# Matmuls of an iota tile under the first loads, a norm gain applied where transposes are copied out, and a first weight chunk loaded in halves

## The chip, the cores and the metric

One NeuronCore of a Trainium2 chip runs the kernel. The metric is the device time of one execution in microseconds. Engines: PE is TensorE (matmuls and transposes), DVE is VectorE, ACT is ScalarE, POOL is GpSimd, and SP mainly issues DMAs. PEld is TensorE loading weights, which overlaps its matmuls. Each engine works through its own queue in order; semaphores make one wait for another.

## The reference

One decoder layer on x of 512 x 1024 in float32. Only its first lines bear on this change:

```python
def rms_norm(x, g):
    xf = x.astype(jnp.float32)
    y = xf * lax.rsqrt(jnp.mean(xf * xf, axis=-1, keepdims=True) + EPS)
    return (y * g.astype(jnp.float32)).astype(x.dtype)

xn = rms_norm(x, norm1_g)
proj = xn @ w_in
(q, k_c, v_c, k_s, v_s, k_w, v_w, g_nsa, conv_b, conv_c, conv_x, gate_a, gate_b) = jnp.split(proj, SPLIT_POINTS, axis=-1)
...
x = x + mixed @ w_out
h = rms_norm(x, norm2_g)
return x + jnp.square(jax.nn.relu(h @ w_up)) @ w_down
```

Behind the projection come sparse attention in three branches, a gated short convolution and a feed-forward part; the change does not touch them.

## The kernel before

The 512 rows of x are four chunks of 128 (`xs[0]` to `xs[3]`). A chunk is normed (`norm_chunk`): ACT squares it and sums along the row, DVE and ACT make 1/sqrt of the mean, and DVE multiplies x by that number and by `g1b`, which is `norm1_g` loaded once into every partition. Then `transpose_chunk` turns it on TensorE, 128 x 128 at a time, into two PSUM banks of four tiles each (`ptr`; the pool has two such buffers). Each bank is copied out twice: ACT writes the rounded high part `xh`, DVE the remainder `xl` = value − `xh`.

Weights come in chunks of 128 x 1024 through the class `Weights`: `load_to` issues the DMA on SP's queue, `split_step` makes half a chunk's high part `w_hi` on ACT or its remainder `w_lo` on DVE. A product is three matmuls (`mm3`): high times high, high times low, low times high.

The first product gives q, chunk by chunk of x: for c = 0 to 3, over four weight chunks (kp = 0 to 3) of two k-tiles each, so 24 matmuls of 512 columns into one PSUM tile `acc`. In the middle of chunk c, behind kp = 1, the code puts the transposes of chunk c + 1 and then the norm of chunk c + 2. Nothing reorders this: the order in the code is the order in each engine's queue. Where two engines read the same PSUM bank, the framework that builds the program makes the later instruction wait for the earlier one.

After the four chunks TensorE goes on with the fifth weight chunk (trace name `acc<-xh,w_hi`) and with the rest of the layer. The line numbers of the profile before are those below; L87 and L89 are the weights' split, L201 and L202 the root and reciprocal, L214 the Square, L218 the scaling, L228 the transposes, L230 and L231 the copies, L237 to L239 the three matmuls.

Of the kernel before, what the change touches and what calls it, by code (L numbers as in the profile page):

```python
# [29 lines left out]

C_POSK, C_POSV, C_GQ, C_GK, C_CW = 0, 16, 32, 33, 36
C_QS, C_SL, C_DD, C_DR, C_DC, C_MK, C_ID = 60, 68, 76, 588, 1100, 1228, 1356
C_ALL = 1484


class Weights:
# [21 lines left out]
    def load_to(self, i):  # L58
        while self.nl <= min(i, len(self.plan) - 1):
            e = self.plan[self.nl]  # L60
            n = e.shape[1]
            t = self.raw.tile([P, WMAX], F32, name="w_raw", tag="w_raw")
            self.nc.sync.dma_start(t[:, :n], e)
            self.loaded[self.nl] = t[:, :n]
            self.nl += 1

# [35 lines left out]
        return self.parts[i]  # L102


def layer(tc, flat, sizes, x, cst, wck, wcv, g1, g2, out):
    nc = tc.nc
    top = ExitStack()

    def pool(name, bufs=1, psum=False, side=None, dram=False):
        kw = dict(name=name, bufs=bufs, reuse_waits="tile")  # L110
        if psum:
            kw["space"] = PSUM
        if dram:
# [79 lines left out]
    junk = sp.tile([P, DM], F32, name="junk")  # L193
    st1 = cp.tile([P, NT], F32, name="st1")
    xh = xtp.tile([P, NKO, S], F32R, name="xh")
    xl = xtp.tile([P, NKO, S], F32R, name="xl")

    def rms_scale(dst, ss, n):

        nc.vector.tensor_scalar(dst, ss, 1.0 / n, EPS, op0=ALU.mult, op1=ALU.add)  # L200
        nc.scalar.activation(dst, dst, AF.Sqrt)  # L201
        nc.vector.reciprocal(dst, dst)  # L202

    def norm_chunk(c):
        ss = st1[:, c : c + 1]
        if c == 0:
            nc.scalar.activation(junk[:, :512], xs[c][:, :512], AF.Square, accum_out=ss)
            nc.vector.tensor_tensor_reduce(
                junk[:, 512:], xs[c][:, 512:], xs[c][:, 512:], 1.0, 0.0,
                op0=ALU.mult, op1=ALU.add, accum_out=warm,  # L210
            )
            nc.vector.tensor_tensor(ss, ss, warm, ALU.add)
        else:
            nc.scalar.activation(junk, xs[c], AF.Square, accum_out=ss)  # L214
        rms_scale(ss, ss, DM)
        for b in range(2):
            v = slice(b * 512, b * 512 + 512)
            nc.vector.scalar_tensor_tensor(  # L218
                xs[c][:, v], xs[c][:, v], ss, g1b[:, v], op0=ALU.mult, op1=ALU.mult
            )  # L220

    def transpose_chunk(psp, src, hi, lo, c):

        for kk in range(2):
            pt = psp.tile([P, 4, P], F32, name="ptr", tag="tr")
            for k in range(4):
                ko = 4 * kk + k
                nc.tensor.transpose(pt[:, k, :], src[:, ko * P : (ko + 1) * P], ident)  # L228
            h = hi[:, 4 * kk : 4 * kk + 4, c * P : (c + 1) * P]
            nc.scalar.activation(h, pt, AF.Copy)  # L230
            nc.vector.tensor_tensor(  # L231
                lo[:, 4 * kk : 4 * kk + 4, c * P : (c + 1) * P], pt, h.bitcast(F32), ALU.subtract
            )

    def mm3(ps, a, b, start, stop, **kw):

        nc.tensor.matmul(ps, a[0], b[0], start=start, stop=False, **kw)  # L237
        nc.tensor.matmul(ps, a[0], b[1], start=False, stop=False, **kw)  # L238
        nc.tensor.matmul(ps, a[1], b[0], start=False, stop=stop, **kw)  # L239
# [106 lines left out]
    pos = [0]  # L346
# [175 lines left out]
    acc = kv_gemm(ci)  # L522
# [24 lines left out]
    acc = kv_gemm(ci)  # L547
# [308 lines left out]
    ps_acc, close_ps_acc = pool("ps_acc3", 4, psum=True, side="left")  # L856
# [456 lines left out]
```

## Time and profile before

| what | value |
|---|---|
| median of 3 runs | 793.21 us (793.15 to 794.42) |
| profiled execution, whole | 794.31 us |
| its span | 792.5 us |
| TensorE busy | 777.7 us, 98% of the span |
| ACT busy, DVE busy, POOL busy | 394.0, 575.4, 88.2 us |

A row of the trace in order of time gives start, duration, engine, line, operation, what is written and read, the shape and how many; the bracket behind it is the idle time of the engine before it and what ended that. A row of a group gives total busy time and the mean of one in ns. Idle time of an engine that nothing waits for costs nothing.

### The profile page before, as it was taken

To read this page: it belongs to the slowest core of one execution; us is meant where nothing else is said; L and a number is where in the kernel's file an instruction comes from. 1 tells how busy PE (TensorE), PEld (TensorE's weight loads), DVE (VectorE), ACT (ScalarE), POOL (GpSimd) and SP (SyncE) were. 2 spreads that over 40 slices of the span, in tenths; PEclk is the share of its full clock that TensorE was granted. 3 is DMA by queue.
4 is the path that set the end of the run, shared out by engine and by line. 5 is a ranking of instruction groups with operands and counts; after the bars stand their busy time and mean duration, and the time that the engine had idled before them with its cause. 6 is when DMAs were issued, how large, how long until landed. Compare 5 with 4: busy or idle time off the path is not lost.

```text
span 792.5 us, 11860 instructions
## 1 busy us (share of the span) xinstructions
PE 777.7 (98%) x4413; PEld 675.5 (85%) x4413; DVE 575.4 (73%) x968; ACT 394.0 (50%) x714; POOL 88.2 (11%) x139
## 2 busy tenths in 40 slices
PE   5999999999999999999999999999999999999998
PEld 4899888888888888888888889987998899889987
DVE  6587787766667466666556668997699579967984
ACT  5545645545555453222233366973565356535641
POOL 0011573233324100000000000000000000000000
PEclk9999999999999999999999999999999999999999
DMA  9346687658757849998999923649999985655562
GB/s 343 124 132 207 171 172 172 212 134 179 194 160 148 175 127 328 310 318 319 336 340 332 357 96 109 228 161 278 264 276 249 274 254 183 199 184 191 189 206 80
DMA packets 49307, 172.56 MB, mean 218 GB/s; under 512 B 5473, under 2 KB 5857, under 8 KB 49249
## 3 DMA queue, kind: packets, MB, share of 16 engines
q1 hardware_dynamic: 42624, 148.14, 54.6%
q0 software_dynamic: 4608, 16.78, 13.5%
q10 hardware_dynamic: 2016, 6.88, 2.5%
q8 instruction: 35, 0.57, 0.3%
q14 instruction: 24, 0.19, 0.1%
HBM read 152.90 MB, written 52.43 MB: 259 GB/s over the span
## 4 chain that ended last, share of the span: by engine, by line
PE 88%; ACT 5%; DVE 3%; DMA 2%; issue 2%; SPq 0%; DVEq 0%; ACTq 0%
PE acc L237 16%; PE acc L239 15%; PE acc L238 15%; PE dacc L237 6%; PE dacc L238 6%; PE dacc L239 6%; PE uacc L237 4%; PE uacc L239 4%; PE uacc L238 4%; PE sc L645 2%; PE ptu L693 2%; ACT w_hi L87 2%; PE uz L239 1%; PE uz L238 1%; PE uz L237 1%
## 5 line engine op out<-in xcount | busy, mean ns | idle before, releaser
L89 DVE TENSOR_TENSOR w_lo<-w_raw,w_hi 128x512 fp32r<-128x512 f32 (+3 forms) x268 | 233.2, 885 | 73.7 <-ACT w_hi L87 73.1
L87 ACT ACTIVATE w_hi<-w_raw 128x512 fp32r<-128x512 f32 (+3 forms) x268 | 201.4, 779 | 91.5 <-PE dacc L239 63.5
L237 PE MATMUL acc<-xh,w_hi 128*128 128x512 f32 x336 | 136.5, 406 | 0.0
L239 PE MATMUL acc<-xh,w_lo 128*128 128x512 f32 x336 | 131.5, 391 | 0.0
L238 PE MATMUL acc<-xl,w_hi 128*128 128x512 f32 x336 | 131.3, 391 | 0.0
L237 PE MATMUL dacc<-w_hi,uh 128*128 128x512 f32 (+1 forms) x228 | 88.0, 386 | 1.1 <-DVE x L1141 1.1
L238 PE MATMUL dacc<-w_lo,uh 128*128 128x512 f32 (+1 forms) x228 | 88.0, 386 | 0.0
L239 PE MATMUL dacc<-w_hi,ul 128*128 128x512 f32 (+1 forms) x228 | 87.9, 385 | 0.0
L239 PEld LDWEIGHTS acc<-xh,w_lo 128*128 128x128 f32 x336 | 63.1, 188 | 14.1
L237 PEld LDWEIGHTS acc<-xh,w_hi 128*128 128x128 f32 x336 | 63.2, 188 | 9.1 <-issue 0.3
L238 PEld LDWEIGHTS acc<-xl,w_hi 128*128 128x128 f32 x336 | 63.3, 188 | 8.2
L237 PE MATMUL uacc<-hA,w_hi 128*128 128x256 f32 x192 | 53.7, 280 | 0.4 <-DVE a L1029 0.4
L657 ACT ACTIVATE p<-p,nst 128x512 f32<-128x512 f32 (+2 forms) x48 | 29.5, 615 | 48.9 <-DVE nst L653 48.7
L238 PE MATMUL uacc<-hA,w_hi 128*128 128x256 f32 x192 | 53.5, 279 | 0.0
L239 PE MATMUL uacc<-hA,w_lo 128*128 128x256 f32 x192 | 53.5, 279 | 0.0
L237 PEld LDWEIGHTS dacc<-w_hi,uh 128*128 128x128 f32 x228 | 42.8, 188 | 10.1 <-ACT w_hi L87 1.5
L238 PEld LDWEIGHTS dacc<-w_lo,uh 128*128 128x128 f32 x228 | 42.8, 188 | 8.7 <-DVE w_lo L89 0.2
L239 PEld LDWEIGHTS dacc<-w_hi,ul 128*128 128x128 f32 x228 | 42.8, 188 | 8.5
L699 DVE TENSOR_TENSOR pt<-ptu,pt 128x384 fp32r<-128x384 f32 (+1 forms) x48 | 28.9, 601 | 21.0 <-ACT pt L698 20.7
L1141 DVE TENSOR_TENSOR x<-x,dacc 128x512 f32<-128x512 f32 (+1 forms) x57 | 36.7, 670 | 9.8 <-PE dacc L239 9.8
L674 POOL TENSOR_SCALAR p<-p,nst 128x512 f32<-128x512 f32 (+2 forms) x48 | 31.9, 673 | 79.6 <-DVE nst L672 45.3
L300 POOL DMA_DIRECT2D td<-w_flat x8 | 6.5, 843 | 304.2 <-DMA td<-w_flat 304.2
(227 smaller groups left out, 1665.8 us busy)
## 6 DMA issues: line engine op xcount, KB each, us to landing
w_raw<-w_flat SPq DMA_DIRECT2D x110, 512.0 KB, 4.8
w_raw<-tu SPq DMA_DIRECT2D x32, 512.0 KB, 4.8
w_raw<-td SPq DMA_DIRECT2D x32, 512.0 KB, 4.7
tu<-w_flat SPq DMA_DIRECT2D x16, 512.0 KB, 6.2
z<-w_flat SPq DMA_DIRECT2D x16, 512.0 KB, 7.0
tu<-w_flat POOLq DMA_DIRECT2D x8, 512.0 KB, 7.7
tu<-tu POOLq DMA_DIRECT2D x8, 512.0 KB, 8.4
td<-w_flat SPq DMA_DIRECT2D x8, 512.0 KB, 5.4
```

Source lines behind the costliest of these rows:

```text
L87: nc.scalar.activation(hi[:, v], t[:, v], AF.Copy)
L89: nc.vector.tensor_tensor(lo[:, v], t[:, v], hi[:, v].bitcast(F32), ALU.subtract)
L237: nc.tensor.matmul(ps, a[0], b[0], start=start, stop=False, **kw)
L238: nc.tensor.matmul(ps, a[0], b[1], start=False, stop=False, **kw)
L239: nc.tensor.matmul(ps, a[1], b[0], start=False, stop=stop, **kw)
L300: nc.gpsimd.dma_start(h[k], h[m], accum_op=ALU.add)
L645: nc.tensor.matmul(ps[:, : b - a], QS[h][:, t], ks[h // 4][:, a:b], start=k == 0, stop=k == 1)
L657: later(1, lambda: nc.scalar.activation(p, p, AF.Exp, scale=-1.0, bias=mn, accum_out=sm))
L674: nc.gpsimd.tensor_scalar(p_of(u, k), p_of(u, k), nst[:, u % 4, 1, k : k + 1], 1.0, op0=ALU.mult, op1=ALU.mult,)
L693: nc.tensor.transpose(pt[:, n : n + P], p_of(u, c)[:, k * P : (k + 1) * P], ident)
L699: later(1, lambda: nc.vector.tensor_tensor(ptl[:, at], pt[:, :n], pth[:, at].bitcast(F32), ALU.subtract))
L1141: nc.vector.tensor_tensor(v, v, ps[:, o : o + n], op)
```

## The change

- Six matmuls of a tile `busy`, filled by an iota on POOL, run on TensorE ahead of the first transposes. Their result is not used.
- `g1b` and its load are gone. `norm1_g` comes as eight columns beside the identity matrix (`ident_g1`); ko-th column, one number per partition. Since a transposed tile has the model dimension on the partitions, the gain is now a scalar per partition: `gain` copies each 128 x 128 tile out by itself, ACT with `scale=g`, DVE as v·g − `xh`.
- The scaling by the norm alone stays on DVE for chunk 0 (`norm_first`, with the mean and EPS folded into other instructions) and goes to POOL for chunks 1 to 3.
- The first weight chunk is loaded in two halves, and its split is interleaved with the copies of chunk 0.
- The transposes of chunk 1 stand behind kp = 2 of chunk 0 instead of kp = 1.

```diff
+    busy = sp.tile([P, 256], mybir.dt.int32, name="busy")
+    nc.gpsimd.iota(busy, [[17749, 256]], base=1065353216, channel_multiplier=7001)
+    busy = busy.bitcast(F32)
...
-    nc.sync.dma_start(g1b, g1.partition_broadcast(P))
-    nc.scalar.dma_start(ident, cst[:, C_ID : C_ID + P])
+    nc.scalar.dma_start(ident_g1, cst[:, C_ID:])
...
+    idle = ps_acc.tile([P, 512], F32, name="acc", tag="acc")
+    for _ in range(6):
+        nc.tensor.matmul(idle[:, :256], busy[:, :P], busy, start=True, stop=True)
...
+        nc.scalar.activation(ss, ss, AF.Sqrt, scale=1.0 / DM, bias=warm)
+        nc.vector.reciprocal(ss, ss)
+        for b in range(2):
+            v = xs[0][:, b * 512 : b * 512 + 512]
+            nc.vector.tensor_scalar(v, v, ss, None, op0=ALU.mult)
...
-            nc.vector.scalar_tensor_tensor(
-                xs[c][:, v], xs[c][:, v], ss, g1b[:, v], op0=ALU.mult, op1=ALU.mult
-            )
+            nc.gpsimd.tensor_scalar(v, v, ss, 1.0, op0=ALU.mult, op1=ALU.mult)
...
-            h = hi[:, 4 * kk : 4 * kk + 4, c * P : (c + 1) * P]
-            nc.scalar.activation(h, pt, AF.Copy)
-            nc.vector.tensor_tensor(
-                lo[:, 4 * kk : 4 * kk + 4, c * P : (c + 1) * P], pt, h.bitcast(F32), ALU.subtract
-            )
+    def gain(pt, c, kos):
+        t = slice(c * P, (c + 1) * P)
+        for ko in kos:
+            v, g, h = pt[:, ko % 4, :], g1t[:, ko : ko + 1], xh[:, ko, t]
+            nc.scalar.activation(h, v, AF.Copy, scale=g)
+            nc.vector.scalar_tensor_tensor(
+                xl[:, ko, t], v, g, h.bitcast(F32), op0=ALU.mult, op1=ALU.subtract
+            )
...
+    norm_first()
+    pt = [transposed(xs[0], kk) for kk in range(2)]
+    for b in range(2):
+        W.split_step()
+        W.split_step()
+        gain(pt[0], 0, (2 * b, 2 * b + 1))
...
     W.split_to(1)
+    gain(pt[1], 0, range(4, NKO))
     norm_chunk(1)
     W.split_to(3)
...
-            if kp == 1 and c + 1 < NT:
-                transpose_chunk(ps_tr, xs[c + 1], xh, xl, c + 1)
+            if kp == (1 if c else 2) and c + 1 < NT:
+                transpose_chunk(c + 1)
```

ACT's queue from the first weights to the norm of chunk 2, before (the brackets name the semaphores that a row waits for, x_122 is chunk 1, x_123 chunk 2, st the norm's numbers, junk the Square's output):

```order
L87 ACTIVATE w_hi<-w_raw 128x512 [waits DMAHW4_49]
L87 ACTIVATE w_hi<-w_raw 128x512
L230 ACTIVATE xh<-ptr 128x4x128 [waits PE_49] x2
L87 ACTIVATE w_hi<-w_raw 128x512 [waits DMAHW5_49]
L87 ACTIVATE w_hi<-w_raw 128x512
L214 ACTIVATE junk,st_152<-x_122 128x1024 [waits DMAHW6_49,Activation_49]
L201 ACTIVATE st_152<-st_152 128x1 [waits DVE_49]
L87 ACTIVATE w_hi<-w_raw 128x512 [waits DMAHW7_49]
L87 ACTIVATE w_hi<-w_raw 128x512
L87 ACTIVATE w_hi<-w_raw 128x512 [waits DMAHW0_49]
L87 ACTIVATE w_hi<-w_raw 128x512
L230 ACTIVATE xh<-ptr 128x4x128 [waits PE_49] x2
```

The first part of the same stretch now (L89 is the weights' split, L245 the copy, L227 the Square):

```order
L89 ACTIVATE w_hi<-w_raw 128x512 [waits DMAHW2_49]
L245 ACTIVATE xh<-ptr,ident_g_134 128x128 [waits DMAHW3_49,PE_49]
L245 ACTIVATE xh<-ptr,ident_g_134 128x128 [waits DVE_49]
L89 ACTIVATE w_hi<-w_raw 128x512 [waits DMAHW4_49]
L245 ACTIVATE xh<-ptr,ident_g_134 128x128 [waits DVE_49] x2
L89 ACTIVATE w_hi<-w_raw 128x512 [waits DMAHW5_49]
L89 ACTIVATE w_hi<-w_raw 128x512
L245 ACTIVATE xh<-ptr,ident_g_134 128x128 [waits PE_49]
L245 ACTIVATE xh<-ptr,ident_g_134 128x128 [waits DVE_49] x3
L227 ACTIVATE junk,st_152<-x_122 128x1024 [waits DMAHW6_49]
L204 ACTIVATE st_152<-st_152 128x1 [waits DVE_49]
```

A bank's single copy has become four, and every copy but the first of a bank waits for DVE's part of the tile before; the Square of chunk 1 now stands behind all eight.

TensorE's queue where chunk 1 is transposed, now (L256 to L258 are the three matmuls, L237 the transposes, x_122 chunk 1):

```order
L256 MATMUL acc<-w_hi,xh 128x512 [waits Activation_49]
L257 MATMUL acc<-w_lo,xh 128x512 [waits DVE_49]
L258 MATMUL acc<-w_hi,xl 128x512
L237 MATMUL ptr<-ident_g_134,x_122 128x128 [waits DMAHW6_49,Pool_49]
L237 MATMUL ptr<-ident_g_134,x_122 128x128 x3
L237 MATMUL ptr<-ident_g_134,x_122 128x128 [waits Pool_49]
L237 MATMUL ptr<-ident_g_134,x_122 128x128 x3
L256 MATMUL acc<-w_hi,xh 128x512 [waits Activation_49]
```

And before, at the same transposes:

```order
L239 MATMUL acc<-w_hi,xl 128x512
L228 MATMUL ptr<-ident,x_122 128x128 [waits DMAHW6_49,DVE_49,PE_49]
L228 MATMUL ptr<-ident,x_122 128x128 x3
L228 MATMUL ptr<-ident,x_122 128x128 [waits DVE_49,PE_49]
L228 MATMUL ptr<-ident,x_122 128x128 x3
L237 MATMUL acc<-w_hi,xh 128x512 [waits Activation_49]
```

They now wait for POOL instead of DVE, and six more matmuls stand ahead of them.

More of the change, by code (lines that the diff above doesn't have):

```diff
@@ L32 @@
 C_QS, C_SL, C_DD, C_DR, C_DC, C_MK, C_ID = 60, 68, 76, 588, 1100, 1228, 1356
-C_ALL = 1484
+C_G1 = C_ID + P
+C_ALL = C_G1 + NKO
 class Weights:
@@ L62, in load_to @@
             t = self.raw.tile([P, WMAX], F32, name="w_raw", tag="w_raw")
-            self.nc.sync.dma_start(t[:, :n], e)
+            for v in [slice(0, 512), slice(512, n)] if self.nl == 0 else [slice(0, n)]:
+                self.nc.sync.dma_start(t[:, v], e[:, v])
             self.loaded[self.nl] = t[:, :n]
@@ L102, in get, with layer @@
         return self.parts[i]
-def layer(tc, flat, sizes, x, cst, wck, wcv, g1, g2, out):
+def layer(tc, flat, sizes, x, cst, wck, wcv, g2, out):
     nc = tc.nc
@@ L165, in layer @@
     xs = [sp.tile([P, DM], F32, name=f"x{c}") for c in range(NT)]
-    g1b = sp.tile([P, DM], F32, name="g1b")
+    busy = sp.tile([P, 256], mybir.dt.int32, name="busy")
+    nc.gpsimd.iota(busy, [[17749, 256]], base=1065353216, channel_multiplier=7001)
+    busy = busy.bitcast(F32)
     cs = qkv.tile([P, C_ID], F32, name="cs")
@@ L173, in layer @@
     qkv.tile([P, 56], F32, name="even")
-    ident = cp.tile([P, P], F32, name="ident")
+    ident_g1 = cp.tile([P, P + NKO], F32, name="ident_g1")
+    ident, g1t = ident_g1[:, :P], ident_g1[:, P:]
     warm = cp.tile([P, 1], F32, name="warm")
-    cp.tile([P, 8], F32, name="even")
     nc.vector.memset(warm, 1.0)
@@ L202, in rms_scale, with norm_first @@
         nc.vector.reciprocal(dst, dst)
+    idle = ps_acc.tile([P, 512], F32, name="acc", tag="acc")
+    for _ in range(6):
+        nc.tensor.matmul(idle[:, :256], busy[:, :P], busy, start=True, stop=True)
+    def norm_first():
+        ss = st1[:, 0:1]
+        nc.scalar.activation(junk[:, :512], xs[0][:, :512], AF.Square, accum_out=ss)
+        nc.vector.tensor_tensor_reduce(
+            junk[:, 512:], xs[0][:, 512:], xs[0][:, 512:], 1.0 / DM, EPS,
+            op0=ALU.mult, op1=ALU.add, accum_out=warm,
+        )
[4 more added lines that the diff above has]
+            nc.vector.tensor_scalar(v, v, ss, None, op0=ALU.mult)
@@ L204, in norm_chunk @@
     def norm_chunk(c):
         ss = st1[:, c : c + 1]
[L206 to L210, printed above, removed]
-            )
-            nc.vector.tensor_tensor(ss, ss, warm, ALU.add)
-        else:
-            nc.scalar.activation(junk, xs[c], AF.Square, accum_out=ss)
+        nc.scalar.activation(junk, xs[c], AF.Square, accum_out=ss)
@@ L215, in norm_chunk, with transposed @@
         rms_scale(ss, ss, DM)
         for b in range(2):
-            v = slice(b * 512, b * 512 + 512)
+            v = xs[c][:, b * 512 : b * 512 + 512]
+            nc.gpsimd.tensor_scalar(v, v, ss, 1.0, op0=ALU.mult, op1=ALU.mult)
+    def transposed(src, kk):
+        pt = ps_tr.tile([P, 4, P], F32, name="ptr", tag="tr")
+        for k in range(4):
+            ko = 4 * kk + k
+            nc.tensor.transpose(pt[:, k, :], src[:, ko * P : (ko + 1) * P], ident)
+        return pt
+    def gain(pt, c, kos):
[3 more added lines that the diff above has]
+            nc.scalar.activation(h, v, AF.Copy, scale=g)
@@ L218, in norm_chunk, with transpose_chunk @@
             nc.vector.scalar_tensor_tensor(
-                xs[c][:, v], xs[c][:, v], ss, g1b[:, v], op0=ALU.mult, op1=ALU.mult
+                xl[:, ko, t], v, g, h.bitcast(F32), op0=ALU.mult, op1=ALU.subtract
             )
-    def transpose_chunk(psp, src, hi, lo, c):
+    def transpose_chunk(c):
         for kk in range(2):
[L225 to L228, printed above, removed]
-            h = hi[:, 4 * kk : 4 * kk + 4, c * P : (c + 1) * P]
-            nc.scalar.activation(h, pt, AF.Copy)
-            nc.vector.tensor_tensor(
-                lo[:, 4 * kk : 4 * kk + 4, c * P : (c + 1) * P], pt, h.bitcast(F32), ALU.subtract
-            )
+            gain(transposed(xs[c], kk), c, range(4 * kk, 4 * kk + 4))
@@ L243, in layer @@
     sq = pre.tile([P, 512], F32, name="sq")
-    norm_chunk(0)
-    W.split_to(0)
-    transpose_chunk(ps_tr, xs[0], xh, xl, 0)
+    norm_first()
[4 more added lines that the diff above has]
+        gain(pt[0], 0, (2 * b, 2 * b + 1))
     load_x(2)
@@ L1293 @@
     cst = np.concatenate(
-        [pos(a["cmp_pos_k"][0]), pos(a["cmp_pos_v"][0]), gq, gk, cw, *_constants()], axis=1
+        [pos(a["cmp_pos_k"][0]), pos(a["cmp_pos_v"][0]), gq, gk, cw, *_constants(), a["norm1_g"][0].reshape(NKO, P).T], axis=1
     )
@@ L1302 @@
         "wcv": wc(a["w_cmp_v"][0]),
-        "g1": np.ascontiguousarray(a["norm1_g"][0]),
         "g2": np.ascontiguousarray(a["norm2_g"][0]),
@@ L1309 @@
     with tile.TileContext(nc) as tc:
-        layer(tc, t["w_flat"], sizes, t["x_in"], t["cst"], t["wck"], t["wcv"], t["g1"], t["g2"], out)
+        layer(tc, t["w_flat"], sizes, t["x_in"], t["cst"], t["wck"], t["wcv"], t["g2"], out)
     r = run_bass_kernel_spmd(nc, [arrays], core_ids=[0])
```

## Prediction

> **What bounds the kernel now.** I read the page's busy table first, then the span cut into stretches, then TensorE's waits, then the start in order of time.
>
> ```profile
> PE 777.7 (98%) x4413; PEld 675.5 (85%) x4413; DVE 575.4 (73%) x968; ACT 394.0 (50%) x714; POOL 88.2 (11%) x139
> ...
> 0.00:8.57 8.57, 0.00 (x1) 0.01 (x1) 2.05 (x8) 2.41 (x5) 0.20 (x4) 1.00 0.77 247
> 8.57:18.69 10.12, 9.76 (x40) 7.43 (x41) 9.38 (x17) 8.59 (x17) 0.00 (x0) 1.00 1.02 416
> 18.69:36.83 18.14, 18.14 (x90) 15.17 (x88) 10.84 (x22) 9.41 (x20) 0.00 (x0) 1.00 0.31 115
> 36.83:792.50 755.67, 749.76 (x4286) 652.93 (x4284) 553.11 (x924) 373.59 (x672) 87.97 (x135) 1.00 0.71 217
> ...
> PE ptr L228 <- DVE x L218: 8.6, 1, 8.6
> PE dacc L237 <- DVE x L1141: 1.1, 1, 1.1
> ```
>
> Each stretch gives its length, then busy time of PE, PEld, DVE, ACT and POOL. TensorE is the bound from 18.69 us to the end. It idles 8.57 us before its first transpose; after that the longest single wait is 1.1 us. So the change can win only at the start, at most some 8 us. It can also lose: whatever makes TensorE wait between 18.69 and 36.83 us, where it is 100% busy while ACT and DVE are half idle, is added in full.
>
> The start, in order of time (start, duration, engine, what; in brackets the idle time before):
>
> ```profile
> 5.11 0.69 DVE L208 CUSTOM_DVE_ANT_0 junk<-x 128x512 f32<-128x512 f32 x1 [4.24 <-DMA x<-x_in]
> 5.73 0.08 DVE L208 DVE_READ_ACCUMULATOR2_ANT warm<- 128x1 f32 x1
> 6.30 0.20 ACT L201 ACTIVATE st<-st 128x1 f32<-128x1 f32 x1 [1.65 <-DVE st L200]
> 6.53 0.16 DVE L202 RECIPROCAL st<-st 128x1 f32<-128x1 f32 x1 [0.27 <-ACT st L201]
> 7.76 1.42 DVE L218 SCALAR_TENSOR_TENSOR x<-x,st,g1b 128x512 f32<-128x512 f32 x2 [1.06 <-DMA g1b<-g]
> 8.57 1.97 PE L228 MATMUL ptr<-ident,x 128*128 128x128 f32 x8 [8.57 <-DVE x L218]
> 8.95 1.15 ACT L87 ACTIVATE w_hi<-w_raw 128x512 fp32r<-128x512 f32 x2 [2.45 <-DMA w_raw<-w_flat]
> 9.61 1.29 DVE L89 TENSOR_TENSOR w_lo<-w_raw,w_hi 128x512 fp32r<-128x512 f32 x2 [0.44 <-ACT w_hi L87]
> 12.10 1.05 ACT L214 ACTIVATE junk<-x 128x1024 f32<-128x1024 f32 x1
> ```
>
> DVE waits 1.06 us for g1b, and ACT 2.45 us for the first weights, which come behind g1b on the same queue. The change takes the first wait away and brings the second's end forward.
>
> **The change part by part.** *g1b's load out, weights in halves.* On SP one issue goes and one comes, so the queue is level. Everything behind g1b lands earlier. I give this no term of its own: what uses it is counted below, where ACT and DVE become later than the data.
>
> *The first norm.* The reduction ends at 5.81 us; root 0.20, reciprocal 0.16 and hand-overs of 0.04 give 6.28 us for the first scaling (7.76 before). That scaling is now a tensor_scalar without g; no row has it at 128x512. It lies between 0.21 us (128x96, below) and 0.75 us (L218, half of 1.42 and its overlap); I take 0.5, nearer the wide row. First transposes at 6.8 us instead of 8.57.
>
> *The iota and its six matmuls.* POOL and TensorE are idle there.
>
> ```profile
> L467 POOL MEMSET VC<- 128x256 f32 x1 | 0.3, 306 | 0.0
> L283 POOL TENSOR_TENSOR q_sb<-q_sb,q_ss 128x512 f32<-128x512 f32 x2 | 3.0, 1512 | 39.3 <-DVE q_ss L202 39.3
> 57.87 1.15 PE L472 MATMUL ptr<-wck_t,ka 128*64 128x64 f32 x16
> ```
>
> The iota takes 0.3 to 1.5 us and ends by 2.8 us at the latest. The plain f32 matmuls of L472 stand 0.06 us apart for 64 columns, so 0.24 for 256 columns and 0.5 on a slow clock: six end by 5.8 us, under the cover of the wait for x. They cost nothing unless each takes over 0.65 us; at 0.8 the transposes would be 0.8 us late. What they could buy is the slow start: the eight transposes took 1.97 us at 8.57 and 1.03 us later. I count only part of that, as ACT sets the pace from here.
>
> *The copies out of the transposes* decide the case. Before, a bank (four transposed 128x128 tiles) was copied by one ACT and one DVE instruction of 512 columns. Now each tile has its own ACT instruction (times g, rounded) and DVE instruction (times g, minus the rounded), and by the built order ACT's copy of tile k+1 waits for DVE's of tile k, since both read the same bank. The trace has this pattern already, at L438 and L439:
>
> ```profile
> 44.35 0.68 ACT L438 ACTIVATE QS<-ptr,gq 64x512 fp32r<-64x512 f32 x1 [4.41 <-PE ptr L432]
> 45.84 0.69 ACT L438 ACTIVATE QS<-ptr,gq 64x512 fp32r<-64x512 f32 x1 [0.81 <-DVE QS L439]
> ...
> 45.06 0.74 DVE L439 SCALAR_TENSOR_TENSOR QS<-ptr,gq,QS 64x512 fp32r<-64x512 f32 x1 [0.37 <-ACT QS L438]
> 46.56 0.76 DVE L439 SCALAR_TENSOR_TENSOR QS<-ptr,gq,QS 64x512 fp32r<-64x512 f32 x1 [0.75 <-ACT QS L438]
> ...
> L499 ACT ACTIVATE KC<-ptr,cs 128x64 fp32r<-128x64 f32 x1 | 0.3, 306 | 0.0
> L438 ACT ACTIVATE QS<-ptr,gq 64x512 fp32r<-64x512 f32 x8 | 5.5, 684 | 10.3 <-DVE QS L439 5.4 <-PE ptr L432 4.8
> L500 DVE SCALAR_TENSOR_TENSOR KC<-ptr,cs,KC 128x64 fp32r<-128x64 f32 x1 | 0.3, 274 | 0.0
> L439 DVE SCALAR_TENSOR_TENSOR QS<-ptr,gq,QS 64x512 fp32r<-64x512 f32 x8 | 6.0, 750 | 3.5 <-ACT QS L438 3.4
> ```
>
> They alternate strictly, with hand-overs of 0.03 and 0.04 us. Between 64 and 512 columns ACT goes from 306 to 684 ns, so 0.36 us at 128; DVE from 274 to 750 ns, so 0.34 us. A pair is 0.36 + 0.03 + 0.34 + 0.04 = 0.77 us. The Trainium skill (PSUM — Partial Sum Buffer, "PSUM bank collisions raise a hardware error") says why: two engines, two readers included, must not touch one bank in the same partitions at once, and a scheduler orders them. The rows agree; by this rule the overlap of rival three below is shut out.
>
> *Chunk 0.* ACT's first copy starts at about 7.7 us (0.64 us behind the transposes on a quick clock, 1.1 on the slow one; I take 0.9). ACT then has copy 0, copy 1 (+0.77), a half of w_hi, copy 2 at 9.3; DVE must do that half's w_lo until 10.05 before its part of copy 2, so copy 3 is at 10.43, the next two w_hi end at 11.85, their w_lo (1.29) at 12.6, DVE's part of copy 4 at 12.94, and copies 5, 6, 7 start at 12.98, 13.75, 14.52. The Square of chunk 1, behind them, starts at 14.8 us; before, at 12.10. What is queued behind it is chunk 1's root and then w_hi of the third weights, so TensorE stands:
>
> ```profile
> 14.75 1.33 PE L228 MATMUL ptr<-ident,x 128*128 128x128 f32 x8 [0.18 <-issue]
> ...
> 21.42 1.03 PE L228 MATMUL ptr<-ident,x 128*128 128x128 f32 x8
> 22.05 1.09 ACT L230 ACTIVATE xh<-ptr 128x512 fp32r<-128x512 f32 x2 [1.86 <-PE ptr L228]
> 23.02 1.06 ACT L214 ACTIVATE junk<-x 128x1024 f32<-128x1024 f32 x1
> 24.39 0.20 ACT L201 ACTIVATE st<-st 128x1 f32<-128x1 f32 x1 [0.22 <-DVE st L200]
> 24.83 1.41 DVE L218 SCALAR_TENSOR_TENSOR x<-x,st,g1b 128x512 f32<-128x512 f32 x2
> 27.76 1.03 PE L228 MATMUL ptr<-ident,x 128*128 128x128 f32 x8
> ...
> L674 POOL TENSOR_SCALAR p<-p,nst 128x512 f32<-128x512 f32 x16 | 11.4, 711 | 62.5 <-DVE nst L672 31.3 <-ACT pt L698 12.4 <-ACT w_hi L87 9.6
> L579 DVE TENSOR_SCALAR gates<-gates 128x96 f32<-128x96 f32 x1 | 0.2, 210 | 0.9 <-ACT gates L578 0.9
> ```
>
> The root follows its Square by 1.37 us and ends at 16.4; w_hi is done at 17.0, w_lo at 17.7, and the six matmuls that now stand ahead of chunk 1's transposes (0.23 us each) end at 18.9. POOL's scaling of chunk 1 is ready at 18.1 (14.8 + 1.81 + two of 0.71), so it hides.
>
> *The loop for chunks 2 and 3.* From one set of transposes to the next, TensorE needs 27.76 − 21.42 = 6.34 us. The new chain: transposes to the first copy 0.64; six pair steps 4.62; two steps from an ACT copy to the next ACT instruction without a wait, 0.36 each, 0.72; Square to scaling 1.81; POOL's first half 0.71 (the nearest row) with two hand-overs of 0.05. Sum 8.60 us. Chunk 2's transposes stand in TensorE's queue ahead of half of chunk 1's matmuls, so these wait too. Chunk 2 is transposed at 18.9 + 8.6 = 27.5 and chunk 3 at 36.1 us, against 27.76: 8.3 us late. From there the order is the old one, and the copies of chunk 3 (one per 0.77 us) run ahead of matmuls that start 3.8 us later and use one per 0.69 us. The later stages shift along.
>
> **The sum:** 8.3 us, to 8.4 with a hand-over more. The profiled execution has a span of 792.5 us and 794.31 us in all, 1.1 us over the median of 793.21; against the median the forecast is 801.6 us. Its own range is 800.0 to 803.0 (copy start and POOL 0.6 to 0.8 us either way).
>
> **Rivals.** One: *a smaller loss.* At the 64-column rows the pair is at least 0.306 + 0.274 + 0.07 = 0.65 us. Some 17 pair steps lie on the path (12 in two loops, 5 in chunk 0): 17 × 0.12 = 2.0 less, 799.6 us. If TensorE's 1.1 us wait at L1141 also went, 798.5.
>
> Two: *the clock falls back.* TensorE stands still from about 13.4 to 17.0 us and from 24.3 to 27.5. Cold work costs double in the trace:
>
> ```profile
> 10.63 0.80 PE L237 MATMUL acc<-w_hi,xh 128*128 128x512 f32 x1
> 12.15 0.58 PE L237 MATMUL acc<-w_hi,xh 128*128 128x512 f32 x1
> ```
>
> These two starts, three matmuls apart, lie 1.52 us apart and later 0.69 (some of it a wait). Six matmuls on half the clock add 1.1 us, and four transposes 0.47, in each of two places: 1.1 + 2 × 0.47 = 2.1 us, 803.7 us. The granted clock reads 1.00 in every stretch, so only durations can show it. For it: the gaps are as long as the slow start was (8.57 to 12.2 us). Against it: no row shows a quick TensorE falling back. The Trainium skill (TensorE: Matmul & The Clock Gate, "What's actually happening") has the clock halve after an idle window of about 3.4 us that runs free of the work, and open after one busy window; by that rule a gap of 3.6 us holds a whole window only now and then.
>
> Three: *not slower.* If ACT and DVE worked on one bank side by side, a tile would cost ACT's 0.36 us or less, the loop 0.64 + 8 × 0.36 + 1.81 + 0.81 = 6.1 us, under TensorE's 6.34, and only the start would count. The Square of chunk 1 would start at 7.7 + 8 × 0.36 + 3 × 0.58 (halves of w_hi, L87) = 12.3 us, its transposes 4.1 us behind it as above, at 16.4; level would be 14.75 (where chunk 1 was transposed) + 6 × 0.23 = 16.1. That gives 793.5 us. It decides where a pair costs under (6.34 − 8.60 + 4.62) / 6 = 0.39 us. L438 and L439 speak against it.
>
> **How the numbers follow.** The forecast gets 0.62, the clock 0.17, the smaller loss 0.13, not slower 0.07, anything else 0.01. The range 798.7 to 804.8 takes in rivals one and two with half a microsecond to a microsecond beside them and leaves out rival three. Slower by over 0.2% (1.6 us, about what a measurement here can tell): 0.92; within: 0.05; faster: 0.03, the part of rival three where the start saves more than 1.6 us.
>
> **What would show it.** In the new profile: first transposes near 6.8 us; ACT's copies with "idle <-DVE xl" before them, 0.77 us apart; TensorE waiting for POOL's x twice, about 3 us and 2 us; the first matmul with the fifth weights at about 45 us instead of 36.83; TensorE dense after that. I am wrong if the copies stand 0.4 us apart, if DVE's part is much cheaper than 0.34 us at 128 columns, or if POOL's scaling takes well over 0.71 us.

## The result, and the profile after

| | before | after |
|---|---|---|
| median | 793.18 us (793.11 to 794.42, 4 runs) | 803.91 us (803.53 to 804.14, 4 runs) |
| profiled execution, whole | 794.31 us | 804.14 us |
| its span | 792.5 us | 802.3 us |

After over before is 1.0125, with a 95% interval of 1.011 to 1.014: the change makes the kernel slower, by 9.8 us from profile to profile. The forecast was 801.6, slower, with a range of 798.7 to 804.8.

The busy table of the page:

```profile
PE 788.2 (98%) x4425; PEld 681.3 (85%) x4425; DVE 577.2 (72%) x984; ACT 400.4 (50%) x738; POOL 93.8 (12%) x146
```

TensorE's busy time is up by 10.5 us, though only 12 records are new, with 5.4 us: part of its work must have become slower. The span in stretches says where (length, busy time of PE, PEld, DVE, ACT, POOL, then the granted clock):

```profile
16.75:20.07 3.32, 3.10 (x7) 2.01 (x8) 3.18 (x4) 1.51 (x3) 2.04 (x2) 0.50 1.02 404
20.07:29.00 8.93, 6.80 (x27) 5.48 (x25) 3.06 (x11) 5.04 (x13) 0.74 (x2) 0.81 0.22 74
29.00:37.55 8.55, 8.38 (x32) 6.41 (x32) 3.72 (x12) 5.05 (x13) 1.36 (x3) 0.80 0.01 4
37.55:46.93 9.38, 9.36 (x44) 7.68 (x45) 5.69 (x14) 6.11 (x16) 0.63 (x1) 1.00 0.00 0
46.93:802.30 755.37, 749.81 (x4286) 652.94 (x4284) 554.15 (x926) 373.61 (x672) 88.17 (x135) 1.00 0.72 218
```

The last stretch, from the first matmul with the fifth weights on, has the old length (755.4 against 755.7) and the old busy time of PE: the whole loss lies ahead of 46.93 us, where that matmul stood at 36.83. Two waits of TensorE are new (in all, how many, the longest, in us):

```profile
PE acc L256 <- ACT w_hi L89: 4.2, 3, 3.4
PE ptr L237 <- POOL x L231: 2.3, 2, 2.1
```

The start in order of time, TensorE first:

```profile
1.24 5.41 PE L209 MATMUL acc<-busy 128*128 128x256 f32 x12 [1.24 <-POOL busy L169]
6.50 1.09 PE L237 MATMUL ptr<-ident_g,x 128*128 128x128 f32 x8
16.75 0.80 PE L256 MATMUL acc<-w_hi,xh 128*128 128x512 f32 x1 [3.38 <-ACT w_hi L89]
...
19.21 0.63 PE L257 MATMUL acc<-w_lo,xh 128*128 128x512 f32 x1
19.64 0.63 PE L258 MATMUL acc<-w_hi,xl 128*128 128x512 f32 x1
20.07 1.91 PE L237 MATMUL ptr<-ident_g,x 128*128 128x128 f32 x8
...
29.00 1.33 PE L237 MATMUL ptr<-ident_g,x 128*128 128x128 f32 x8 [2.14 <-POOL x L231]
...
37.55 1.33 PE L237 MATMUL ptr<-ident_g,x 128*128 128x128 f32 x8 [0.15 <-POOL x L231]
46.93 0.39 PE L256 MATMUL acc<-xh,w_hi 128*128 128x512 f32 x1
```

The first transposes are 2 us earlier and quick (1.09 us instead of 1.97). By the third weights all of it is gone: TensorE stands still for 3.38 us, and then works at half pace, matmuls 0.43 us apart instead of 0.23, chunk 1's transposes in 1.91 us. All four runs of the changed kernel read a mean granted clock of 0.991 to 0.993, which fits such a stretch in each of them. ACT and DVE of the same stretch show what it waits for:

```profile
7.25 0.35 ACT L245 ACTIVATE xh<-ptr,ident_g 128x128 fp32r<-128x128 f32 x1
...
14.62 1.05 ACT L227 ACTIVATE junk<-x 128x1024 f32<-128x1024 f32 x1
15.98 0.20 ACT L204 ACTIVATE st<-st 128x1 f32<-128x1 f32 x1 [0.22 <-DVE st L203]
16.09 2.17 ACT L89 ACTIVATE w_hi<-w_raw 128x512 fp32r<-128x512 f32 x4
21.16 0.37 ACT L245 ACTIVATE xh<-ptr,ident_g 128x128 fp32r<-128x128 f32 x1 [2.90 <-PE ptr L237]
21.94 0.37 ACT L245 ACTIVATE xh<-ptr,ident_g 128x128 fp32r<-128x128 f32 x1 [0.42 <-DVE xl L246]
22.73 0.37 ACT L245 ACTIVATE xh<-ptr,ident_g 128x128 fp32r<-128x128 f32 x1 [0.42 <-DVE xl L246]
...
21.56 0.35 DVE L246 SCALAR_TENSOR_TENSOR xl<-ptr,ident_g,xh 128x128 fp32r<-128x128 f32 x1 [1.63 <-ACT xh L245]
22.34 0.35 DVE L246 SCALAR_TENSOR_TENSOR xl<-ptr,ident_g,xh 128x128 fp32r<-128x128 f32 x1 [0.44 <-ACT xh L245]
```

ACT's copies start 0.79 us apart, each idle for 0.42 us on DVE's `xl` and DVE in turn for 0.44 us on `xh`: strict alternation in one bank.

### The profile page after: what moved, and what is told of

It reads as the page before. It is cut to its first block, busy times and chain, and to the rows that moved or that the text cites. A ratio compares the mean times of both kernels' runs of the same rounds, so it can differ in the third digit from the quotient of the medians.

```text
span 802.3 us, 11932 instructions
## 1 busy us (share of the span) xinstructions
PE 788.2 (98%) x4425; PEld 681.3 (85%) x4425; DVE 577.2 (72%) x984; ACT 400.4 (50%) x738; POOL 93.8 (12%) x146
## 4 chain that ended last, share of the span: by engine, by line
PE 86%; ACT 4%; issue 3%; DVE 3%; DMA 2%; POOL 0%; SPq 0%; ACTq 0%; DVEq 0%; POOLq 0%
PE acc L256 15%; PE acc L258 15%; PE acc L257 15%; PE dacc L256 6%; PE dacc L257 6%; PE dacc L258 6%; PE uacc L256 4%; PE uacc L258 4%; PE uacc L257 4%; PE sc L668 2%; PE ptu L716 2%; ACT w_hi L89 1%; PE uz L258 1%; PE uz L256 1%; PE uz L257 1%
## 5 line engine op out<-in xcount | busy, mean ns | idle before, releaser
L89 ACT ACTIVATE w_hi<-w_raw 128x512 fp32r<-128x512 f32 (+3 forms) x268 | 201.2, 779 | 88.5 <-PE dacc L258 62.6
L256 PE MATMUL acc<-xh,w_hi 128*128 128x512 f32 x336 | 136.5, 406 | 0.0
L258 PE MATMUL acc<-xh,w_lo 128*128 128x512 f32 x336 | 131.5, 391 | 0.0
L256 PE MATMUL dacc<-w_hi,uh 128*128 128x512 f32 (+1 forms) x228 | 88.0, 386 | 0.7 <-DVE x L1164 0.7
L258 PE MATMUL dacc<-w_hi,ul 128*128 128x512 f32 (+1 forms) x228 | 87.9, 385 | 0.0
L258 PEld LDWEIGHTS acc<-xh,w_lo 128*128 128x128 f32 x336 | 63.1, 188 | 14.1
L256 PEld LDWEIGHTS acc<-xh,w_hi 128*128 128x128 f32 x336 | 63.2, 188 | 9.2 <-issue 0.3
L256 PE MATMUL uacc<-hA,w_hi 128*128 128x256 f32 x192 | 53.7, 280 | 0.5 <-DVE a L1052 0.5
L258 PE MATMUL uacc<-hA,w_lo 128*128 128x256 f32 x192 | 53.5, 279 | 0.0
L256 PEld LDWEIGHTS dacc<-w_hi,uh 128*128 128x128 f32 x228 | 42.8, 188 | 9.7 <-ACT w_hi L89 1.1
L258 PEld LDWEIGHTS dacc<-w_hi,ul 128*128 128x128 f32 x228 | 42.8, 188 | 8.5
```

What stands on the lines that cost most here:

```text
L89: nc.scalar.activation(hi[:, v], t[:, v], AF.Copy)
```

## The experiments

All are edits of the changed kernel unless said otherwise. This table, put together from the traces, shows the points that the text goes by, in us: first transposes (T0), those of chunks 1 to 3 (T1 to T3), and the first matmul with the fifth weights (W5).

| kernel | T0 | T1 | T2 | T3 | W5 | median | ratio to before, 95% interval |
|---|---|---|---|---|---|---|---|
| before | 8.57 | 14.75 | 21.42 | 27.76 | 36.83 | 793.18 | |
| forecast of after | 6.8 | 18.9 | 27.5 | 36.1 | 45.1 | 801.6 | |
| after | 6.50 | 20.07 | 29.00 | 37.55 | 46.93 | 803.91 | 1.0125, 1.011 to 1.014 |
| wide copies, no gain | 6.69 | 14.34 | 19.31 | 25.66 | 34.72 | 791.87 | 0.9974, 0.9965 to 0.9982 |
| banks in turn | 6.52 | 16.23 | 22.53 | 29.16 | 38.45 | 795.27 | 1.0017, 1.0008 to 1.0026 |
| ACT's four, then DVE's four | 6.74 | 15.72 | 21.04 | 27.66 | 36.72 | 793.54 | 0.9990, 0.9981 to 0.9999 |
| gaps filled, six and three | 6.52 | 18.96 | 27.44 | 36.24 | 45.60 | 802.99 | 1.0113, 1.0097 to 1.0128 |
| gaps filled, seven and seven | 6.77 | 19.14 | 27.63 | 36.16 | 45.50 | 802.97 | 1.0113, 1.0099 to 1.0128 |
| T1 behind kp = 1 | 6.78 | 17.12 | 27.17 | 35.72 | 45.05 | 801.80 | 1.0094, 1.0080 to 1.0108 |
| scaling on DVE | 6.54 | 19.90 | 28.57 | 36.98 | 46.11 | 803.39 | 1.0116, 1.0100 to 1.0131 |
| g's copy by one-row matmuls | 6.95 | 14.81 | 20.10 | 26.45 | 35.51 | 792.21 | 0.9976, 0.9967 to 0.9985 |
| warm-up with one row | 6.82 | 20.44 | 29.37 | 37.91 | 47.26 | 804.23 (one run) | |
| g's copy by full-row matmuls | 8.45 | 15.92 | 21.22 | 27.56 | 36.63 | 794.47 | 1.0002, 0.9994 to 1.0011 |
| g's copy by one-row matmuls, four warm-ups | 8.65 | 16.51 | 21.84 | 28.18 | 37.24 | 793.92 | 0.9994, 0.9984 to 1.0005 |
| the warm-up alone, in the kernel before | 7.80 | 14.00 | 20.67 | 27.01 | 36.08 | 793.28 | 0.9994, 0.9986 to 1.0003 |

The kernel before took 793.88 to 794.25 us (medians) beside these, so ratios compare better than medians. The five points come from one profiled execution of each kernel and can shift between executions by up to three quarters of a microsecond or so: in the last row W5 is 0.75 us earlier than before because `g1b` came in sooner (first scaling at 7.00 instead of 7.76 us), and that edit changes no load.

**Wide copies, no gain.** `gain` becomes one copy a bank and engine.

```diff
-            nc.scalar.activation(h, v, AF.Copy, scale=g)
-            nc.vector.scalar_tensor_tensor(
-                xl[:, ko, t], v, g, h.bitcast(F32), op0=ALU.mult, op1=ALU.subtract
-            )
+        h = xh[:, 4 * kk : 4 * kk + 4, c * P : (c + 1) * P]
+        nc.scalar.activation(h, pt, AF.Copy)
+        nc.vector.tensor_tensor(
+            xl[:, 4 * kk : 4 * kk + 4, c * P : (c + 1) * P], pt, h.bitcast(F32), ALU.subtract
+        )
```

> The changed kernel, but each bank of four transposed tiles is copied by one ACT and one DVE instruction of 512 columns, as before the change; norm1_g is left out, all else stays. Theory A (the alternation tile by tile in one bank is the cost): in the chunk loop the Square follows the transposes by 1.6 us again (21.42 to 23.02 before the change), scaling 1.8 later, POOL's half 0.7, so 4.2 us against TensorE's 6.34, and TensorE sets the pace. Chunk 0: ACT needs about 3.4 us from 7.25 for two copies and four halves of w_hi, Square of chunk 1 near 10.7, chunk 1's transposes at 14.4 to 15.0 behind kp = 2, where 16.1 would be level with before; first matmul with the fifth weights at 35 to 36 us instead of 46.93, whole time 791 to 793 us. Theory B (the loss lies in POOL's scaling, or in the new order of chunk 0): it stays above 798 us, with TensorE still waiting for POOL's x.

Theory A holds: 791.87 us, with W5 slightly ahead of the expected 35 to 36. T1 is at 14.34, TensorE no longer waits for POOL, and all the rest of the change together, without any gain, is worth 2 us. So the copies, with the slow stretches that they bring about, cost 12 us (46.93 against 34.72 at W5), more than the whole loss.

**Banks in turn.** The same small copies in another order.

```diff
+        pts = [transposed(xs[c], kk) for kk in range(2)]
+        gain(pts, c, (0, 4, 1, 5, 2, 6, 3, 7))
```

> The changed kernel with the same 128x128 copies, each times its gain, but taken from the two banks in turn (tiles 0, 4, 1, 5, 2, 6, 3, 7), so that ACT can be in one bank while DVE is in the other. Theory A (same bank alternation): ACT's copies stand 0.40 us apart instead of 0.79; the loop falls from 8.9 and 8.55 us to about 0.70 + 7 x 0.40 + 0.36 + 1.81 + 0.81 = 6.5 us, chunk 0 gains about 1.8 us, the whole time is 797 to 798.5 us. Theory B (small instructions cost this much wherever their data lie: start-up and hand-over of each): the copies stay about 0.79 us apart and the time at 803.9 us.

ACT, in order of time:

```profile
16.86 3.17 ACT L245 ACTIVATE xh<-ptr,ident_g 128x128 fp32r<-128x128 f32 x8 [1.40 <-PE ptr L237]
19.93 1.05 ACT L227 ACTIVATE junk<-x 128x1024 f32<-128x1024 f32 x1
```

Eight copies now take 3.17 us, 0.40 each, as against 0.79 a pair. The same instructions, in the same number, cost 8.5 us less at W5: theory B falls. The time came out 1.7 us under the expected 797 to 798.5, and the slow stretches of TensorE went too (its granted clock is 1.00 throughout), which the expectation had not counted.

**ACT's four, then DVE's four.** The loop over a bank's tiles is split in two: first all of ACT's copies, then all of DVE's.

> The changed kernel, gain per 128x128 tile as before, but ACT copies all four tiles of a bank and only then DVE takes its four; two first halves of weights still stand between the two banks of chunk 0. Theory A (the strict alternation, not the number of instructions): ACT's copies run 0.26 us apart (two took 0.63 us when nothing stood between), ACT is through a chunk 2.9 us behind its transposes, so the loop's chain is about 5.5 us and TensorE's 6.3 sets the pace; Square of chunk 1 near 11.1 us instead of 14.62, chunk 1's transposes near 15.5, first matmul with the fifth weights near 36.4, time level with the kernel before within 1 us. Theory B (eight pairs of small instructions cost 0.7 to 0.8 us a pair however ordered): above 799 us.

Groups of this kernel:

```profile
L245 ACT ACTIVATE xh<-ptr,ident_g 128x128 fp32r<-128x128 f32 x32 | 8.8, 382 | 5.1 <-PE ptr L237 5.1
L248 DVE SCALAR_TENSOR_TENSOR xl<-ptr,ident_g,xh 128x128 fp32r<-128x128 f32 x32 | 8.7, 344 | 5.5 <-ACT xh L245 5.5
```

ACT no longer waits for DVE at all, 32 small copies with a gain give 0.999 of the time before, and W5 is at 36.72 where 36.4 was expected. Instructions of 128 columns are not dear; handing one bank to and fro for each is.

**Gaps filled.** More matmuls of the iota tile where TensorE stood still, six before the third weights and three before T2, then seven and seven.

```diff
+            if c == 0 and kp == 2:
+                fill(7)
...
+                if c == 1:
+                    fill(7)
                 transpose_chunk(c + 1)
```

> The changed kernel with more matmuls of the iota tile, six before the first matmul with the third weights and three before the transposes of chunk 2, where TensorE stood still for 3.38 and 2.13 us. Theory C (the clock falls back in these gaps, as in the second rival of the prediction): the transposes of chunk 1 take 1.0 to 1.3 us instead of 1.91, the matmuls after 16.75 and after 29.0 stand 0.23 apart at once, and the time falls by 1.5 to 2 us to about 802.2 us. Theory D (the slow stretch has another cause, such as late operands): durations stay, the time is 803.9 us, or up to 1 us more where the added matmuls outlast the gap.

> The changed kernel with seven matmuls of the iota tile before the first matmul with the third weights and seven before the transposes of chunk 2. With six and three, the clock held through the first gap (chunk 1's transposes at 18.96 us, lasting 1.04) but not through the second, which had grown to 3.5 us (transposes 1.78 us, next matmuls 0.43 apart). Theory C (the clock falls back where TensorE stands still): filled, chunk 2's transposes last 1.0 to 1.1 us too, chunk 3 is transposed near 35.9 us, the first matmul with the fifth weights comes at 45.0 us (46.93 without fill, 45.60 with six and three) and the time is about 802.0 us; what is left of the loss, some 8.2 us, is the copies. Theory D (something else slows these matmuls): as with six and three, 803 us.

With seven and seven:

```profile
13.32 3.18 PE L286 MATMUL acc<-busy 128*128 128x256 f32 x14
...
19.14 1.04 PE L237 MATMUL ptr<-ident_g,x 128*128 128x128 f32 x8
...
24.12 3.18 PE L286 MATMUL acc<-busy 128*128 128x256 f32 x14
27.63 1.33 PE L237 MATMUL ptr<-ident_g,x 128*128 128x128 f32 x8 [0.33 <-POOL x L231]
```

The clock stays at 1.00, T1's transposes take 1.04 us, and W5 is 1.4 us earlier, not 1.9. Theory C holds in the trace; in the times it isn't resolved, as 1.0113 and 1.0125 have overlapping intervals. The 1.33 us at T2 are no slow clock: the matmuls behind stand 0.23 us apart. Six and three held the first gap only (T2's transposes still took 1.78 us), and gave all but 0.1 us of the gain.

**T1 behind kp = 1 again.**

```diff
-            if kp == (1 if c else 2) and c + 1 < NT:
+            if kp == 1 and c + 1 < NT:
```

> The changed kernel with the transposes of chunk 1 back behind kp = 1 instead of kp = 2. Theory A (from chunk 1's transposes on, the chain copies - Square - POOL sets the pace, not TensorE): the transposes start when POOL's first half of x is ready, 17.7 us instead of 20.07, the loops stay 8.6 to 8.9 us, the first matmul with the fifth weights comes about 2.4 us earlier and the time is 801.5 us. Rival (TensorE must do the six matmuls anyway, so their place does not matter): 803.9 us.

Theory A: 801.8 us, and W5 1.9 us earlier (2.4 expected), with the same matmuls on TensorE. T1 gained 2.95 us, but T1 to T2 took 10.05: DVE did the `w_lo` of the third and fourth weights, until 19.8 us, ahead of chunk 1's `xl`, and ACT's second copy waited 1.48 us for it.

**Scaling on DVE.**

```diff
-            nc.gpsimd.tensor_scalar(v, v, ss, 1.0, op0=ALU.mult, op1=ALU.mult)
+            nc.vector.tensor_scalar(v, v, ss, None, op0=ALU.mult)
```

> The changed kernel with the scaling by the norm on DVE for all chunks instead of POOL for chunks 1 to 3 (0.44 us a half by the first chunk, 0.68 on POOL). Theory F (POOL and DVE slow each other when both work, 1.16 us a half and 0.80 us a w_lo side by side, against 0.68 and 0.62 alone; and POOL's second half holds up the last four transposes of a chunk): w_lo back at 0.62, the sets of transposes that wait last 1.0 to 1.1 us instead of 1.33, loops 8.3 us instead of 8.55, but chunk 1's transposes 0.1 to 0.4 later, as the scaling now stands ahead of w_lo on DVE; time 0.3 to 0.8 us under the changed kernel, still over 802.5. Rival (POOL's share is free): same time, transposes still 1.33.

DVE and TensorE of this kernel:

```profile
16.07 0.88 DVE L231 TENSOR_SCALAR x<-x,st 128x512 f32<-128x512 f32 x2
16.86 2.49 DVE L91 TENSOR_TENSOR w_lo<-w_raw,w_hi 128x512 fp32r<-128x512 f32 x4
...
36.98 1.09 PE L237 MATMUL ptr<-ident_g,x 128*128 128x128 f32 x8 [0.23 <-DVE x L231]
46.11 0.39 PE L256 MATMUL acc<-xh,w_hi 128*128 128x512 f32 x1
```

In the changed kernel POOL and DVE worked side by side there:

```profile
16.73 3.20 DVE L91 TENSOR_TENSOR w_lo<-w_raw,w_hi 128x512 fp32r<-128x512 f32 x4 [0.35 <-ACT w_hi L89]
...
16.48 2.31 POOL L231 TENSOR_SCALAR x<-x,st 128x512 f32<-128x512 f32 x2 [15.29 <-DVE st L205]
28.25 1.36 POOL L231 TENSOR_SCALAR x<-x,st 128x512 f32<-128x512 f32 x2 [9.47 <-DVE st L205]
```

The same two groups in the changed kernel, each as shortest/median/longest in ns:

```profile
L231 POOL TENSOR_SCALAR x<-x,st x2: 691/1164/1637, 16.5 to 17.2; 128x512 f32<-128x512 f32 x2
L91 DVE TENSOR_TENSOR w_lo<-w_raw,w_hi x4: 678/829/1094, 16.7 to 19.2; 128x512 fp32r<-128x512 f32 x4
```

So the expected "1.16 us a half and 0.80 us a w_lo" are means: one half kept 0.69 us and the other took 1.64, and the `w_lo` lie between 0.68 and 1.09. Side by side, some instructions are held up and others not at all.

Theory F holds in the trace: 2.49 against 3.20 us for four `w_lo`, T3's transposes 1.09 against 1.33, T3 to W5 9.13 against 9.38. W5 is 0.8 us earlier, but not all of that is POOL's share: TensorE's half clock lies elsewhere here (11.9 to 22.1 and 29.0 to 32.4 us), and T2's transposes took 1.64 us in it. By the times the kernel can't be told from the changed one. The later T1 did not come.

**A version that beats both.** Wide copies, g multiplied into x on DVE, g's copy in all partitions by two one-row matmuls into PSUM, scaling of chunk 1 behind the third weights' split.

```diff
+    for b in range(2):
+        nc.tensor.matmul(gb[b], ones, g1r[:, b * 512 : b * 512 + 512], start=True, stop=True)
...
+            nc.vector.scalar_tensor_tensor(v, v, ss, g_half(c, b), op0=ALU.mult, op1=ALU.mult)
```

> A version meant to beat both: the wide copies of before, norm1_g multiplied into x on DVE again, but its copy in every partition is made by two TensorE matmuls (a row of ones times a 4 KB row of g, in the idle start) instead of a 512 KB load; the halves of the first weights, the warm-up and the place of chunk 1's transposes stay as changed. With the wide copies alone and no gain the time was 2.0 us under the kernel before (first matmul with the fifth weights at 34.72). Theory: first scaling waits for nothing if the two matmuls end by 6 us, 0.3 us lost by the dearer scaling, up to 0.5 us won as DVE's w_lo no longer runs beside POOL (0.80 against 0.62 us each); fifth weights at 34.5 to 35.0 us, 1.8 to 2.2 us under the kernel before. Rival: the matmuls of g are late or slow (plain f32, about 1.8 us each cold), the start slips by 1 us and little is won.

792.21 us, 0.24% under the kernel before (0.15 to 0.33%); W5 was 0.5 to 1 us later than expected, because the start was slow:

```profile
1.23 2.08 PE L214 MATMUL acc<-busy 128*128 128x256 f32 x4 [1.23 <-POOL busy L169]
3.24 3.78 PE L216 MATMUL acc<-g1r,ones 1*128 1x512 f32 x4
6.95 2.03 PE L249 MATMUL ptr<-ident_g,x 128*128 128x128 f32 x8
```

TensorE was busy from 1.23 us on, yet the transposes take 2.03 us. Three runs asked why. The first gives the warm-up matmuls of the changed kernel one row instead of 128:

> The changed kernel with its six warm-up matmuls taking one row (one partition) of the iota tile instead of 128. Theory E: they last as long as before, but the transposes behind them take 1.9 to 2.0 us instead of 1.09 and the first matmuls stand 0.43 us apart. Rival (any matmul keeps the clock up): transposes 1.1 to 1.3 us, as with 128 rows.

```profile
1.23 5.48 PE L209 MATMUL acc<-busy 1*128 1x256 f32 x12 [1.23 <-POOL busy L169]
6.82 1.97 PE L237 MATMUL ptr<-ident_g,x 128*128 128x128 f32 x8
```

Theory E: the same length of work, 5.48 us, and a cold clock behind it. The time, 804.23 us in one run, is hardly longer than with the quick start (803.53 to 804.14). The other two tried to mend the version, by full-row matmuls of ones with a diagonal of g, and by four warm-up matmuls instead of two:

> As the version with g's copy made on TensorE, but by matmuls whose left operand is 128 x 128 ones and whose right operand is the identity times g's columns (made on POOL, eight of 128x128), so all 128 rows of TensorE work instead of one; four warm-up matmuls ahead. Theory E (matmuls of one row do not keep the clock up: with them the first transposes took 2.03 us and matmuls stayed 0.43 apart until 11.5 us, though TensorE was busy from 1.2 us on): the transposes take 1.0 to 1.3 us, matmuls 0.23 apart from the start, fifth weights' first matmul at 34.7 to 35.1 instead of 35.51, time 0.4 to 0.8 us under that version. Rival (the start was slow for another reason, or POOL's eight products come later than 6 us): transposes still 1.9 us, or the first scaling late; time no better.

> The version that beat both (g's copy made by two one-row matmuls), with four warm-up matmuls of 128 rows ahead of them instead of two. Theory E (only matmuls that use the rows bring the clock up, after 3.2 to 5.4 us here): four last to about 4.8 us, the one-row matmuls then run partly on the quick clock and end near 6.9 us as before (3.78 us for four records when slow), and since the clock fell back only some 3 us after TensorE had stopped in the changed kernel, the transposes at 6.9 us last 1.1 instead of 2.03; first matmul with the fifth weights at 34.7 to 35.2 instead of 35.51 and 0.3 to 0.8 us less time. Rival: the one-row stretch counts as idle soon enough, or the four cold ones push g's copy to 8 us: no better, or up to 1 us worse.

Neither did. With full rows the transposes were quick, but POOL's products took 0.41 us each (3.31 for eight), g came late, W5 was at 36.63 (in the quickest of its 11 runs) and the ratio is 1.0002 (0.9994 to 1.0011). With four warm-up matmuls the one-row ones still ran cold, from 4.95 to 8.72 us, T0 slipped to 8.65 and the ratio is 0.9994 (0.9984 to 1.0005): the rival. Its runs reach from 791.26 to 795.32 us. The three quickest (791.26 twice and 792.34) read a mean granted clock of 0.997 to 0.998, the others 0.999 or 1.000. I take this for a clock that opened early in these three and fell back later, as the column reads 1.00 in a cold start and shows only a fall-back; no trace of them is on record, so this is not shown.

**The warm-up alone.** This run is an edit of the kernel before: it adds the iota tile and eight of its matmuls, nothing else.

```diff
+    idle = ps_acc.tile([P, 512], F32, name="acc", tag="acc")
+    for _ in range(8):
+        nc.tensor.matmul(idle[:, :256], busy[:, :P], busy, start=True, stop=True)
```

It was expected to win 0.5 to 1 us if the slow first matmuls were on the path, and nothing if ACT and DVE set the pace of chunk 0. The second holds: the first transposes take 1.32 us instead of 1.97, but from T0 to W5 it is 28.28 us against 28.26 before, and the time is the same. So the warm clock by itself wins nothing in the kernel before.

## Why the prediction was right or wrong

**The alternation: right, and nearly to size.** Forecast 0.77 us a pair; measured 0.79 (copy 0.37, DVE's part 0.35, of the forecast 0.36 and 0.34). The Square of chunk 1 came at 14.62 (14.8), the loop from T2 to T3 takes 8.55 (8.60), and the order "last in ACT's queue, so the third weights come late" is the chain seen. Three experiments that change only the copies take 8.5 to 12.2 us off W5.

**T1 at 18.9: failed, by the clock.** Measured 20.07. With the first gap filled it is 18.96 and 19.14, so the rows were right and the condition that the clock stays up was wrong. The second rival, given 0.17, is what happened on top of the forecast. It was priced at 2.1 us in two places (the terms add up to 2.04); the traces give 1.4. The forecast's own range, 800.0 to 803.0, misses 803.91; the stated one holds because it took this rival in. The first place cost its 1.1 us, and 0.4 more by slow transposes ahead of the first copy (T1 to T2 8.93 instead of 8.5). The second cost nothing: slow matmuls behind T2 only used up TensorE's wait before T3, which is 0.15 us here and 1.75 in the filled kernel. So the two waits for POOL's x, forecast at about 3 and 2 us, were 2.14 and 0.15.

**"The granted clock reads 1.00 in every stretch, so only durations can show it": half wrong.** It read 1.00 in the cold start, and does so after, but the fall-back stands plainly in that column, 0.50 from 16.75 us on. **"A whole window only now and then"**, drawn from the Trainium skill (TensorE: Matmul & The Clock Gate, "What's actually happening"), misjudged the chance. The first fall agrees with that rule, as TensorE was busy for only 0.12 of the 3.4 us ahead of it. The second does not: there it was busy for 1.30, so no whole idle window was needed (last section).

**POOL's second half: a term left out.** The forecast counted the first half, 0.71 us (0.68 measured). The last four transposes of a chunk wait for the second: 1.33 us instead of 1.03 to 1.09, and T3 to W5 is 9.38 where the old 9.07 was assumed. That is 0.3 us. "POOL's scaling takes well over 0.71 us", a sign of being wrong, did come for chunk 1, whose two halves took 2.31 us beside DVE's `w_lo`; they ended at 18.79, ahead of T1, and cost nothing there.

**The sum.** Forecast W5 36.83 + 8.3 = 45.1; measured 46.93. The 1.8 us are 1.2 (T1) + 0.3 (T1 to T2, 8.93 for 8.60: the slow first copy) + 0.4 (T3 to W5, 9.38 where 45.1 − 36.1 leaves 9.0: POOL's second half and rounding), less 0.05 from T2 to T3.

**The start.** First transposes at 6.50 (6.8), mostly because chunk 0 came earlier: DVE's half of the sum started at 4.63 instead of 5.11 us. Against that, the root with its folded mean took 0.29 us for 0.20; the halves of the scaling cost 0.44 us, not 0.5. The kernel before with the warm-up alone has that start at 4.71, so the arrival may be nothing that the change did. The six matmuls were mis-sized: 0.9 us each, in two records of 0.45, where at most 0.5 was given and 0.65 named as the point from which they cost. The row they were priced from, L472, was misread: its 16 records belong to eight matmuls, two to each (only `l` = 0 to 7 read `ka`), so 0.06 us was half a matmul. That this had no price is luck: the iota, allowed until 2.8 us, ended at 1.19, so the six end at 6.65, level with the transposes, and x was ready just then.

**The other rivals.** A smaller loss and no loss at all both needed a cheaper pair; 0.79 excludes them. "Side by side" is what the banks in turn allow, at 0.40 us a tile, near the 0.39 that the third rival named as its point: that kernel lands within 0.3% of before.

## What to carry to other kernels

When a wide PSUM copy is cut into per-tile copies that two engines share, count hand-overs within a bank, not instructions: let one engine finish the bank, or give each its own bank, and the same instructions hide. Ask next what stands last in the queue of the engine that does the copies, since that is what comes late. And where a forecast leaves TensorE waiting for some 2 us or more, price the slow matmuls behind the gap once, at the place where nothing slack follows.

## What the runs showed of the hardware

The granted clock of TensorE falls to 0.50 after partly idle stretches. In the changed kernel it changes at about 16.7, 23.5, 30.3 and 33.7 us, that is on a beat of some 3.4 us or twice that. Two beats of the changed kernel that ended in a fall, and the slow one behind the second, cut as stretches:

```profile
13.25:16.67 3.42, 0.12 (x1) 0.00 (x0) 1.30 (x5) 2.46 (x7) 0.19 (x1) 1.00 1.01 415
26.91:30.32 3.41, 1.30 (x9) 1.07 (x10) 1.22 (x4) 2.18 (x6) 1.36 (x2) 1.00 0.00 0
30.32:33.73 3.41, 3.41 (x10) 2.66 (x9) 1.67 (x6) 1.73 (x5) 0.00 (x0) 0.50 0.02 7
```

The kernel with T1 behind kp = 1, a beat that ended in a fall and one that did not:

```profile
11.50:14.91 3.41, 1.52 (x6) 0.86 (x5) 2.10 (x6) 1.73 (x6) 0.00 (x0) 1.00 1.02 421
31.98:35.39 3.41, 1.97 (x9) 1.31 (x7) 1.07 (x5) 2.68 (x7) 0.42 (x1) 1.00 0.01 2
```

A beat with TensorE busy for 0.12, 1.30 or 1.52 of 3.4 us was followed by half clock, one with 1.97 was not. The line is not sharp: with the scaling on DVE a beat with 2.16 us busy also ended in a fall, at about 11.9 us. What is counted isn't settled. Busy time alone it is not, since matmuls of one row, 5.48 us long, leave the clock cold.

POOL and DVE hold each other up: side by side one of two halves of POOL's scaling took 1.64 us and a `w_lo` up to 1.09, where 0.69 and 0.68 are the shortest of the same groups.
